# Transposes of h, of the memory and of most of x1 and x2 by whole VectorE instructions and a regrouping through DRAM; the first gate chunk's weights in pairs

## The chip, the cores and the metric

The kernel runs on one core of one Trainium2 chip. The metric is device microseconds (us) of one execution. TensorE does matrix products and transposes (PE in the profile, PEld for its weight loads); VectorE is DVE, ScalarE is ACT, GpSimd is POOL, and SyncE (SP) only issues transfers (SPq is its queue). SBUF is the memory on the chip, PSUM the accumulators of PE, DRAM the memory beside the chip.

## What is computed

One decoder layer on x (256 tokens, width 2048) with a memory of 256 tokens:

```python
x = x + 0.5 * swiglu(rms_norm(x, ffn1_norm), ffn1_gate, ffn1_up, ffn1_down)     # d_ff = 5632
proj = rms_norm(x, mix_norm) @ w_in                  # q, k, v of three groups of heads
mn = rms_norm(mem, mem_norm); mk, mv = mn @ w_mem_k, mn @ w_mem_v
x = x + concat(forgetting_attention, sliding_window_attention, memory_attention) @ w_out
x = x + 0.5 * swiglu(rms_norm(x, ffn2_norm), ffn2_gate, ffn2_up, ffn2_down)
# swiglu(x, g, u, d) = (silu(x @ g) * (x @ u)) @ d
```

All is float32. A product of activations and weights is made of three faster matmuls (type fp32r): both operands are split into a high part and the rest, and hi·hi, hi·lo and lo·hi are summed.

## The kernel before, in words

**Weights.** `project` makes one output chunk of 512 columns: for each pair of K tiles (2 x 128 rows, `KB = 2`) `load_w` takes a tile `raw` (4 buffers) and issues its load on SP (L218, 512 KB), ACT casts it to `hi` (L220, 3 buffers), DVE subtracts to get `lo` (L221, 3 buffers), and `mm_rows` issues 12 matmuls of 128x512 (L283 to L285). So a raw buffer comes free when DVE has made `lo`, and a hi buffer when PE has done with the pair three before. A load is issued four pairs ahead, a cast three.

**Activations.** A product needs its left side with the width on the partitions: x0T, memT, x1T, x2T (16 K tiles each, hi and lo) and hT (44 K tiles). For x0T, memT, x1T and x2T `transpose_chunk` makes a chunk of 4 K tiles: 8 PE transposes of 128x128 into PSUM (L240, tiles tp_...), then ACT and DVE scale by the norm's gain and split into hi and lo (L249, L250). For hT `quad_transposes` makes 16 DVE transposes of 32 partitions each (L263), then hi and lo follow (L225, L226).

**Order.** The program is written in the order of the products: first FFN (gate and up alternating over 11 chunks, names ga, ua; then down over 4 column chunks, da), the memory's projections mk and mv, the chunks of w_in (mq to fvb), w_out (wo, 4 column chunks), second FFN (gb, ub, db). Work beside the products is written as generators in `Lanes`; after every pair `lanes.tick()` lets each go on to its next `yield`, and the number yielded is how many ticks it waits. The compiler's scheduler then places instructions on each engine by its own estimates, so the order on an engine is not quite that of the code. The memory's transposes run in the down product, those of x1 in mk, those of x2 in w_out and the first gate chunk of the second FFN.

**Opening.** The first gate chunk (`project_first`) starts before x has arrived: K tiles 0 to 3 have one raw buffer each, the others go in pairs, and PE transposes of x0T stand between the products. Its order is written by hand.

Of the kernel before, what the change touches and what calls it, by code (L numbers as in the profile page):

```python
# [16 lines left out]
P = 128  # L17
# [63 lines left out]
def hybrid_layer(ctx, tc, x, mem, ffn1_norm, ffn1_gate, ffn1_up, ffn1_down, mix_norm, mem_norm,  # L81
# [23 lines left out]
    lanes = Lanes()  # L105

# [103 lines left out]
    def load_w(w, k0, nk, c0, width, name, raw=None):  # L210
        there = raw is not None
        if not there:
            raw = wpool.tile([P, KB, 512], F32, tag="raw", bufs=4, name=f"raw_{name}")
# [106 lines left out]
    def project_first(acc, aT, w, before, ready, name):  # L320


        batches = [(k, 1) for k in range(4)] + [(k, KB) for k in range(4, NK, KB)]

        def load(i):
            k, b = batches[i]
            before(k)
            return load_w(w, k, b, 0, 512, f"{name}_{k}", None if k else first_w)

        nxt = load(0)  # L330
        for i, (k, b) in enumerate(batches):
            (wh, wl), nxt = nxt, load(i + 1) if i + 1 < len(batches) else None
            ready(k)
            if k == 0:
                for a, v in ((0, wh), (1, wh), (0, wl)):
                    for t in range(NT):
                        nc.tensor.matmul(acc[:, t, :], aT[:, 0, a, t * P:(t + 1) * P], v[:, 0, :],
                                         start=a == 0 and v is wh, stop=False)
            else:
                for j in range(b):  # L340
                    mm_rows(acc, aT, k + j, wh[:, j, :], wl[:, j, :], False, k + j == NK - 1)
            lanes.tick()


    def ffn(xT, before, ready, stats, wg, wu, wd, after, last, name):


        with tc.tile_pool(name=f"h_{name}", bufs=1, reuse_waits="tile") as hpool, \
                tc.tile_pool(name=f"ht_{name}", bufs=2, reuse_waits="tile") as htmp:
            hT = hpool.tile([P, NF, 2, SEQ], F32R, name=f"hT_{name}")  # L350

            def transpose_h(j, h):
# [3 lines left out]
                for b in range(2):  # L356
                    f = slice(4 * j + 2 * b, 4 * j + 2 * b + 2)
                    split(hT[:, f, 0, :], hT[:, f, 1, :], raw[:, 2 * b:2 * b + 2, :])
                    yield 1

            rstd = None
            for j in range(DFF // 512):
                acc = psum("acc", f"g{name}{j}")
                if j == 0 and ready:
                    project_first(acc, xT, wg, before, ready, f"{name}g{j}")
# [14 lines left out]
                lanes.run(f"hT{name}{j}", transpose_h(j, g))  # L380
# [4 lines left out]

            for c in range(4):
# [65 lines left out]
    def mem_raw(c):  # L452
        raw = wpool.tile([P, NT, 512], F32, tag="raw", bufs=4, name=f"mraw{c}")
        nc.sync.dma_start(raw, memv[:, :, c * 512:(c + 1) * 512])
        return raw

    def mem_stages_T(c):
        def stages(tag):
            raw = mem_raw(c)
            yield 3  # L460
            yield from transpose_chunk(lambda: memTs[0], lambda: raw, 4 * c, 4, G_MEM, f"mem{c}")(tag)
            square_sums(ssm, raw, c)
        return stages

    def after1(c, t, c0, width):
        if t == 0:
            return
        if c == 0:
            memTs.append(r1.tile([P, NK, 2, SEQ], F32R, tag="r1", name="memT"))
        if c < 2:  # L470
            for i in (2 * c, 2 * c + 1):
                lanes.put(f"memT{i}", mem_stages_T(i), ("consts",))
        square_sums(ss1, xchunk(c), c)
# [5 lines left out]
    ffn(x0T, before0, ready0, stats0, gate1, up1, down1, after1, False, "a")  # L479
    memT = memTs[0]  # L480
    lanes.finish("memT3")


    with tc.tile_pool(name="mix", bufs=1, reuse_waits="tile") as mx, \
# [44 lines left out]
        lanes.finish("x1T3", "mk")  # L529
# [70 lines left out]
        def logits(tag, h0, qT, kT, fox, name):  # L600
# [89 lines left out]
        def mem_stages(tag, h0):  # L690
# [10 lines left out]
            s = mt.tile([P, 2, 512], F32, tag="s", name=f"ss_{name}")  # L701
# [78 lines left out]
        for c in range(4):  # L780
# [3 lines left out]
            else:  # L784
# [7 lines left out]
        lanes.finish("bT2")  # L792
# [12 lines left out]
    ffn(x2T, lambda k: lanes.finish("bT3") if k == 12 else None, None, stats2, gate2, up2, down2, store, True, "b")  # L805
# [31 lines left out]
```

## Time and profile before

| | us |
|---|---|
| median of 3 runs (1813.83 to 1814.91) | 1814.04 |
| the profiled execution | 1814.06 |
| its span in the trace | 1812.3 |
| PE busy | 1802.0 (99%) |
| DVE busy | 1091.0 (60%) |
| ACT busy | 845.0 (47%) |
| main DMA queue, share of 16 engines | 62.7% |

The span is from the first to the last instruction of the trace; the profiled execution's own time is 1.8 us longer. Busy times count an engine as busy from the start of an instruction to its end; matmuls overlap, so a PE that is busy all the time may still be slower or faster than another.

### The profile page before, as it was taken

The numbers are of one execution on the slowest core, as the hardware profiler recorded it, in microseconds if no ns is written. First come the engines' busy times: TensorE is split into PE (matmuls) and PEld (weight loads), VectorE is DVE, ScalarE is ACT, GpSimd is POOL, SyncE is SP. The second block draws the span as 40 slices with busy tenths as digits, with TensorE's granted clock in tenths as the row PEclk, the third lists the DMA queues.
The fourth block names the chain that finished last, engine by engine and source line by source line (L and its number), as shares of the span: only waits on it lengthen the run. The fifth ranks groups of instructions, "written<-read, shape, count | busy, mean of one in ns | idle before, by whom it ended". The sixth has DMA issues, their size and how long they took to land.

```text
span 1812.3 us, 21918 instructions
## 1 busy us (share of the span) xinstructions
PE 1802.0 (99%) x8258; PEld 1517.1 (84%) x8258; DVE 1091.0 (60%) x1483; ACT 845.0 (47%) x1149; POOL 10.8 (1%) x31
## 2 busy tenths in 40 slices
PE   8999999999999999999999999999999999999998
PEld 7888888888888888888999888888888888888887
DVE  5666666666655454645665455666666666654443
ACT  6444444444445443557666454444444444433332
POOL 2000000000000000000000000000000000000000
PEclk9999999999999999999999999999999999999999
DMA  7666666666666666465656556666666666656664
GB/s 233 194 191 195 196 190 195 195 191 194 193 194 208 191 213 197 164 174 158 181 153 186 175 179 193 190 194 194 189 193 194 196 196 195 191 195 205 204 205 128
DMA packets 183145, 344.54 MB, mean 190 GB/s; under 512 B 11194, under 2 KB 28928, under 8 KB 182912
## 3 DMA queue, kind: packets, MB, share of 16 engines
q1 hardware_dynamic: 181488, 340.49, 62.7%
q0 software_dynamic: 528, 1.22, 0.3%
q10 hardware_dynamic: 1024, 1.45, 0.3%
q8 instruction: 64, 1.05, 0.2%
q14 instruction: 41, 0.34, 0.1%
HBM read 341.01 MB, written 2.11 MB: 189 GB/s over the span
## 4 chain that ended last, share of the span: by engine, by line
PE 98%; DMA 1%; ACT 1%; DVE 1%; issue 0%; ACTq 0%; DVEq 0%
PE ua L284 4%; PE da L284 4%; PE da L283 4%; PE gb L284 4%; PE ub L283 4%; PE ub L284 4%; PE gb L283 4%; PE da L285 4%; PE ua L285 4%; PE gb L285 4%; PE ub L285 4%; PE ua L283 4%; PE db L285 4%; PE db L284 4%; PE db L283 4%; PE ga L283 4%
## 5 line engine op out<-in xcount | busy, mean ns | idle before, releaser
L221 DVE TENSOR_TENSOR lo_bd<-raw_bd,hi_bd 128x1024 fp32r<-128x1024 f32 x88 | 107.8, 1225 | 116.6 <-ACT hi_bd L220 116.5
L221 DVE TENSOR_TENSOR lo_ad<-raw_ad,hi_ad 128x1024 fp32r<-128x1024 f32 x88 | 107.8, 1225 | 111.2 <-ACT hi_ad L220 111.0
L221 DVE TENSOR_TENSOR lo_bu<-raw_bu,hi_bu 128x1024 fp32r<-128x1024 f32 x88 | 107.8, 1225 | 110.2 <-ACT hi_bu L220 110.2
L221 DVE TENSOR_TENSOR lo_au<-raw_au,hi_au 128x1024 fp32r<-128x1024 f32 x88 | 107.8, 1225 | 104.9 <-ACT hi_au L220 104.9
L220 ACT CAST hi_bd<-raw_bd 128x1024 fp32r<-128x1024 f32 x88 | 92.8, 1055 | 145.5 <-PE db L285 139.8
L220 ACT CAST hi_bg<-raw_bg 128x1024 fp32r<-128x1024 f32 x88 | 92.9, 1055 | 144.5 <-PE gb L285 87.0
L220 ACT CAST hi_ag<-raw_ag 128x1024 fp32r<-128x1024 f32 (+1 forms) x89 | 92.6, 1040 | 139.0 <-PE ga L285 83.2
L220 ACT CAST hi_ad<-raw_ad 128x1024 fp32r<-128x1024 f32 x88 | 92.7, 1053 | 131.9 <-PE da L285 108.0
L220 ACT CAST hi_bu<-raw_bu 128x1024 fp32r<-128x1024 f32 x88 | 92.7, 1054 | 105.6 <-PE ub L285 78.9
L220 ACT CAST hi_au<-raw_au 128x1024 fp32r<-128x1024 f32 x88 | 92.5, 1053 | 103.0 <-PE ua L285 79.1
L283 PE MATMUL da<-hi_ad,hT_a 128*128 128x512 f32 x352 | 137.5, 391 | 0.0
L284 PE MATMUL ua<-lo_au,x0T 128*128 128x512 f32 x352 | 137.2, 390 | 0.3 <-DVE lo_au L221 0.3
L284 PE MATMUL da<-lo_ad,hT_a 128*128 128x512 f32 x352 | 137.2, 390 | 0.0
L283 PE MATMUL gb<-hi_bg,x2T 128*128 128x512 f32 x352 | 137.2, 390 | 0.0
L285 PE MATMUL da<-hi_ad,hT_a 128*128 128x512 f32 x352 | 137.2, 390 | 0.0
L284 PE MATMUL gb<-lo_bg,x2T 128*128 128x512 f32 x352 | 137.1, 390 | 0.0
L285 PE MATMUL ua<-hi_au,x0T 128*128 128x512 f32 x352 | 137.1, 390 | 0.0
L285 PE MATMUL gb<-hi_bg,x2T 128*128 128x512 f32 x352 | 137.1, 390 | 0.0
L284 PE MATMUL ub<-lo_bu,x2T 128*128 128x512 f32 x352 | 137.1, 390 | 0.0
L285 PE MATMUL ub<-hi_bu,x2T 128*128 128x512 f32 x352 | 137.1, 390 | 0.0
L283 PE MATMUL ua<-hi_au,x0T 128*128 128x512 f32 x352 | 137.1, 390 | 0.0
L283 PE MATMUL ub<-hi_bu,x2T 128*128 128x512 f32 x352 | 137.1, 390 | 0.0
(476 smaller groups left out, 4008.7 us busy)
## 6 DMA issues: line engine op xcount, KB each, us to landing
raw_au<-in_ffn_up_dram SPq DMA_DIRECT2D x88, 512.0 KB, 4.5
raw_ad<-in_ffn_down_dram SPq DMA_DIRECT2D x88, 512.0 KB, 4.6
raw_bg<-in_ffn_gate_dram SPq DMA_DIRECT2D x88, 512.0 KB, 4.4
raw_bu<-in_ffn_up_dram SPq DMA_DIRECT2D x88, 512.0 KB, 4.4
raw_bd<-in_ffn_down_dram SPq DMA_DIRECT2D x88, 512.0 KB, 4.7
raw_ag<-in_ffn_gate_dram SPq DMA_DIRECT2D x86, 512.0 KB, 4.4
raw_wo<-in_w_out_dram SPq DMA_DIRECT2D x16, 512.0 KB, 3.8
raw_mk<-in_w_mem_k_dram SPq DMA_DIRECT2D x8, 512.0 KB, 3.4
```

The source lines that it names most:

```text
L220: nc.scalar.copy(h, r)
L221: nc.vector.tensor_tensor(out=l, in0=r, in1=h.bitcast(F32), op=ALU.subtract)
L283: nc.tensor.matmul(acc[:, t, :w], hi, wh, start=first, stop=False)
L284: nc.tensor.matmul(acc[:, t, :w], hi, wl, start=False, stop=False)
L285: nc.tensor.matmul(acc[:, t, :w], lo, wh, start=False, stop=last)
```

## The change

For hT (22 chunks), memT (4), x1T (4) and chunks 0 to 2 of x2T, a chunk of 256 tokens x 512 columns is turned in four steps. `turn_out`: two DVE transposes of 128x512, one for each 128 tokens, turn every 32x32 block in place and write the blocks side by side to `turn_out_...`; then four DMAs on SP (32 partitions, pieces of 512 bytes) write them to a DRAM tile `far_...`. `turn_in`: one DMA on SP reads them back to `turn_in_...` with rows of 2 KB, the width on the partitions. Then ACT and DVE scale and split from SBUF (`scaled`, or `split` for hT). Chunk 3 of x2T and all of x0T stay with PE. The memory's raw chunks move from the raw buffers of the weights to buffers of the FFN's own, and the memory's and three of x1's turns run beside the down product (`turns_a`).

In the opening, K tiles 0 to 3 now share two pair buffers (`first_w`, four loads on SP), are split one at a time, and the norm's gain goes first on ACT's queue; x's loads and transposes stand in another order (`XLOAD`, `XTRANS`).

```diff
-    first_w = wpool.tile([P, KB, 512], F32, tag="raw", bufs=4, name="first_w")
-    nc.scalar.dma_start(first_w[:, 0, :], gate1[0:P, 0:512])
     nc.scalar.dma_start(graw1, ffn1_norm[0].rearrange("(k p) -> k p", p=P))
     load_x(nc.scalar, 2, 2)
+    first_w = [wpool.tile([P, KB, 512], F32, tag="raw", bufs=4, name=f"first_w{i}") for i in range(2)]
+    for k in range(2 * KB):
+        nc.sync.dma_start(first_w[k // KB][:, k % KB, :], gate1[k * P:(k + 1) * P, 0:512])
+    load_x(nc.sync, 4, 2)
...
-    def quad_transposes(dst, src):
-
-        sv = src.rearrange("p t (k b s) -> p b t k s", b=4, s=32)
-        dv = dst.rearrange("p k (t a s) -> p a t k s", t=NT, s=32)
+    def turn_out(tmp, src, name):
+        for t in range(NT):
+            tc.keep_in_program_order(
+                nc.vector.transpose(
+                    out=tmp.rearrange("p (t b k s) -> p t k b s", b=4, t=NT, s=32)[:, t],
+                    in_=src[:, t, :].rearrange("p (k b f) -> p k b f", b=4, f=32)))
+        yield 2
+        far = dpool.tile([NT, 4, 32, 4, P], F32, name=f"far_{name}")
         for a in range(4):
-            for b in range(4):
-                tc.keep_in_program_order(
-                    nc.vector.transpose(out=dv[32 * b:32 * b + 32, a], in_=sv[32 * a:32 * a + 32, b]))
-                if b % 2:
-                    yield 1
+            nc.sync.dma_start(far[:, :, :, a, :].rearrange("t b f n -> f (t b) n"),
+                              tmp[32 * a:32 * a + 32, :].rearrange("f (c n) -> f c n", n=P))
+        yield 2
+        return far
+
+    def turn_in(dst, far):
+        return dst.rearrange("p (t n) -> p t n", t=NT), far.rearrange("t b f a n -> (b f) t (a n)")
...
+    def turn_chunk(xT, src, tile, k0, g0, name):
+        far = yield from turn_out(tile(f"out_{name}"), src, name)
+        raw = tile(f"in_{name}")
+        nc.sync.dma_start(*turn_in(raw, far))
+        yield 3
+        yield from scaled(xT, raw, k0, g0)
...
             def transpose_h(j, h):
 
-                raw = htmp.tile([P, 4, SEQ], F32, tag="raw", bufs=1, name=f"hr_{name}{j}")
-                yield from quad_transposes(raw, h)
+                far = yield from turn_out(turn_tile(f"out_{name}{j}"), h, f"{name}{j}")
+                raw = turn_tile(f"in_{name}{j}")
+                nc.sync.dma_start(*turn_in(raw, far))
+                yield 3
...
-            lanes.put(f"bT{c}", transpose_chunk(lambda: x2T, lambda c=c: xchunk(c), 4 * c, 4, G_FFN2,
-                                                f"x2_{c}"))
+            if c < 3:
+                lanes.run(f"bT{c}", turn_chunk(x2T, xchunk(c), turn_tile, 4 * c, G_FFN2, f"x2{c}"))
+            else:
+                lanes.put(f"bT{c}", transpose_chunk(lambda: x2T, lambda: xchunk(3), 12, 4, G_FFN2, "x2_3"))
```

The built order shows the change at three places. The first is SP's queue in a gate chunk of the first FFN (raw_ag_10 is the load of K tiles 10 and 11 of the gate's weights); before, the loads follow one another:

```order
L218 DMA raw_ag_10_689<-in_ffn_gate_dram 128x2x512
L218 DMA raw_ag_12_709<-in_ffn_gate_dram 128x2x512
L218 DMA raw_ag_14_729<-in_ffn_gate_dram 128x2x512
L218 DMA raw_au_0_753<-in_ffn_up_dram 128x2x512
L218 DMA raw_au_2_773<-in_ffn_up_dram 128x2x512
```

Now the four stores of the turned h and the load that reads them back stand between them:

```order
L218 DMA raw_ag_10_682<-in_ffn_gate_dram 128x2x512
L268 DMA far_a_639<-turn_out_a_600 32x8x128 x4
L218 DMA raw_ag_12_700<-in_ffn_gate_dram 128x2x512
L218 DMA raw_ag_14_718<-in_ffn_gate_dram 128x2x512
L410 DMA turn_in_a_680<-far_a_639 128x2x512
L218 DMA raw_au_0_742<-in_ffn_up_dram 128x2x512
L218 DMA raw_au_2_762<-in_ffn_up_dram 128x2x512
```

The loads of the pairs from raw_ag_12 on have come behind the stores, and those from raw_au_0 on behind the load that waits for the stores to land.

The second place is DVE at the end of the third column chunk of the first down product (da is that chunk's accumulator, lo_ad_2 the second weight pair of the next chunk). Before:

```order
L221 TENSOR_TENSOR lo_ad_0_5073<-raw_ad_0_5071,hi_ad_0_5072 128x1024
L221 TENSOR_TENSOR lo_ad_2_5091<-raw_ad_2_5089,hi_ad_2_5090 128x1024
L391 SCALAR_TENSOR_TENSOR x_sb<-da_4621,x_sb 128x512 x2
L221 TENSOR_TENSOR lo_ad_4_5109<-raw_ad_4_5107,hi_ad_4_5108 128x1024
L221 TENSOR_TENSOR lo_ad_6_5127<-raw_ad_6_5125,hi_ad_6_5126 128x1024
```

Now:

```order
L221 TENSOR_TENSOR lo_ad_0_5010<-raw_ad_0_5008,hi_ad_0_5009 128x1024
L450 SCALAR_TENSOR_TENSOR x_sb<-da_4552,x_sb 128x512 x2
L262 STREAM_TRANSPOSE turn_out_x_5026<-x_sb 128x4x4x32 x2
L221 TENSOR_TENSOR lo_ad_2_5031<-raw_ad_2_5029,hi_ad_2_5030 128x1024
L221 TENSOR_TENSOR lo_ad_4_5049<-raw_ad_4_5047,hi_ad_4_5048 128x1024
```

The two transposes of x1's chunk 2 have come in, and lo_ad_2, which stood ahead of the addition to x, has come behind both.

The third place is SP in the third column chunk of w_out (raw_wo_10 is the load of its sixth pair). Before:

```order
L218 DMA raw_wo_6_8480<-in_w_out_dram 128x2x512
L218 DMA raw_wo_8_8502<-in_w_out_dram 128x2x512
L218 DMA raw_wo_10_8520<-in_w_out_dram 128x2x512
L218 DMA raw_wo_12_8538<-in_w_out_dram 128x2x512
L218 DMA raw_wo_14_8556<-in_w_out_dram 128x2x512
```

Now, with the turns of x2's chunks 0 (far_x_8314) and 1 (far_x_8384):

```order
L218 DMA raw_wo_6_8389<-in_w_out_dram 128x2x512
L268 DMA far_x_8314<-turn_out_x_8275 32x8x128 x4
L218 DMA raw_wo_8_8411<-in_w_out_dram 128x2x512
L268 DMA far_x_8384<-turn_out_x_8343 32x8x128
L295 DMA turn_in_x_8364<-far_x_8314 128x2x512
L268 DMA far_x_8384<-turn_out_x_8343 32x8x128 x3
L218 DMA raw_wo_10_8435<-in_w_out_dram 128x2x512
L218 DMA raw_wo_12_8457<-in_w_out_dram 128x2x512
L295 DMA turn_in_x_8433<-far_x_8384 128x2x512
L218 DMA raw_wo_14_8475<-in_w_out_dram 128x2x512
L218 DMA raw_wo_0_8499<-in_w_out_dram 128x2x512
```

The first store of chunk 1, the load that reads chunk 0 back and three more stores have come ahead of raw_wo_10, and the load that reads chunk 1 back ahead of raw_wo_14.

## Rows read from the trace of the kernel before

**Rows 1.** Windows: length; busy us of PE, PEld, DVE, ACT, POOL; clock; DMA share; GB/s.
```profile
40.00:560.00 520.00, 520.00 (x2296) 430.97 (x2295) 338.86 (x413) 225.78 (x239) 0.00 (x0) 1.00 0.65 194
560.00:740.00 180.00, 180.00 (x815) 149.31 (x814) 92.28 (x108) 83.72 (x110) 0.00 (x0) 1.00 0.63 202
...
1020.00:1100.00 80.00, 80.00 (x372) 66.58 (x371) 47.74 (x63) 40.30 (x61) 0.00 (x0) 1.00 0.59 182
1100.00:1780.00 680.00, 680.00 (x3002) 563.66 (x3001) 413.60 (x477) 289.03 (x295) 0.00 (x0) 1.00 0.65 196
```

**Rows 2.** Timeline, ACT, in a gate chunk (start us, us, what [idle before]): weight casts.
```profile
60.78 1.05 ACT L220 CAST hi_ag<-raw_ag 128x1024 fp32r<-128x1024 f32 x1 [1.66 <-PE ga L285]
63.50 1.06 ACT L220 CAST hi_ag<-raw_ag 128x1024 fp32r<-128x1024 f32 x1 [1.67 <-PE ga L285]
```

**Rows 3.** The chain of waits (start us, us, what): blocks of PE transposes.
```profile
563.95 0.87 PE tp_mem L240 x8
...
739.21 0.87 PE tp_x L240 x8
...
1068.36 0.87 PE tp_x L240 x8
```

**Rows 4.** Groups by line, PE (busy us, mean ns | idle before): the memory's transposes.
```profile
L240 PE MATMUL tp_mem<-ident,mraw 128*128 128x128 f32 x32 | 4.1, 272 | 0.0
```

**Rows 5.** Groups by line and shape, DVE.
```profile
L221 DVE TENSOR_TENSOR lo_ag<-raw_ag,hi_ag 128x1024 fp32r<-128x1024 f32 x86 | 105.3, 1225 | 45.9 <-ACT hi_ag L220 44.9
L263 DVE STREAM_TRANSPOSE hr_a<-gsa 32x256 f32<-32x256 f32 x176 | 76.7, 436 | 3.2
...
L377 DVE SCALAR_TENSOR_TENSOR gsa<-ua,y_x,gsa 128x512 f32<-128x512 f32 x22 | 15.5, 747 | 4.5 <-PE ua L285 4.5
```

**Rows 6.** Groups by line and shape, ACT.
```profile
L225 ACT CAST hT_a<-hr_a 128x512 fp32r<-128x512 f32 x22 | 12.5, 618 | 0.0
...
L249 ACT ACTIVATE x2T<-tp_x,gT 128x256 fp32r<-128x256 f32 x16 | 7.4, 464 | 0.4
```

**Rows 7.** DMA issues (KB each, median us from issue to landing).
```profile
raw_ag<-in_ffn_gate_dram SPq DMA_DIRECT2D x86, 512.0 KB, 4.4
...
raw_mk<-in_w_mem_k_dram SPq DMA_DIRECT2D x8, 512.0 KB, 3.4
```

**Rows 8.** The tile out_dram: issues on SP (min/median/max ns); landing of the stores.
```profile
L799 SPq DMA_DIRECT2D out_dram<-x_sb x5: 356/357/361, 1628.5 to 1809.2; - x5
...
DMA to landing us min/median/max: 2.0/5.1/5.7
```

**Rows 9.** DMA queues: packets, MB, share of 16 engines.
```profile
q1 hardware_dynamic: 181488, 340.49, 62.7%
```

**Rows 10.** Timeline, DVE, at the end of the first down projection's third chunk.
```profile
676.69 1.29 DVE L391 SCALAR_TENSOR_TENSOR x_sb<-da,x_sb 128x512 f32<-128x512 f32 x2 [0.41 <-PE da L285]
677.89 1.22 DVE L221 TENSOR_TENSOR lo_ad<-raw_ad,hi_ad 128x1024 fp32r<-128x1024 f32 x1
```

**Rows 11.** Timeline, DVE, at the end of the first column chunk of w_out.
```profile
1033.94 1.23 DVE L788 TENSOR_TENSOR x_sb<-wo,x_sb 128x1024 f32<-128x1024 f32 x1 [0.41 <-PE wo L285]
```

**Rows 12.** The chain of waits in the first gate chunk.
```profile
1.29 4.40 DMA graw<-in_ffn_norm_dram
...
9.35 7.49 DMA raw_ag<-in_ffn_gate_dram
...
18.00 1.23 DVE lo_ag L221
```

**Rows 13.** Timeline, PE, in the first gate chunk and at its end.
```profile
7.36 2.04 PE L337 MATMUL ga<-hi_ag,x0T 128*128 128x512 f32 x4 [0.24 <-DVE x0T L246]
...
15.24 0.44 PE L240 MATMUL tp_x<-ident,x_sb 128*128 128x128 f32 x2 [0.32 <-DVE x0T L250]
...
19.68 0.44 PE L240 MATMUL tp_x<-ident,x_sb 128*128 128x128 f32 x2 [0.85 <-DVE x0T L250]
...
36.20 0.50 PE L284 MATMUL ua<-lo_au,x0T 128*128 128x512 f32 x1 [0.26 <-DVE lo_au L221]
```

More of the change, by code (lines that the diff above doesn't have):

```diff
@@ L208, in rsqrt, with load_w @@
         return yf
[L210 to L213, printed above, removed]
+    def load_w(w, k0, nk, c0, width, name):
+        raw = wpool.tile([P, KB, 512], F32, tag="raw", bufs=4, name=f"raw_{name}")
         hi = wpool.tile([P, KB, 512], F32R, tag="hi", bufs=3, name=f"hi_{name}")
@@ L318, in project_end, with project_first, split_one, batch @@
         lanes.tick()
[L320 to L341, printed above, removed]
+    def project_first(acc, aT, w, x_tiles, ordered, name):
+        pairs = [[wpool.tile([P, KB, 512], F32R, tag=tag, bufs=3, name=f"{tag}_{name}_{2 * i}")
+                  for tag in ("hi", "lo")] for i in range(2)]
+        def split_one(k):
+            h, l = (t[:, k % KB, :] for t in pairs[k // KB])
+            split(h, l, first_w[k // KB][:, k % KB, :])
+            return h, l
+        def batch(k):
+            if k in XLOAD:
+                load_x(nc.sync, *XLOAD[k])
+            return load_w(w, k, KB, 0, 512, f"{name}_{k}")
+        x_tiles(0)
+        wh, wl = split_one(0)
+        x_tiles(1)
+        for a, v in ((0, wh), (1, wh), (0, wl)):
+            for t in range(NT):
+                nc.tensor.matmul(acc[:, t, :], aT[:, 0, a, t * P:(t + 1) * P], v, start=a == 0 and v is wh,
+                                 stop=False)
+        one = split_one(1)
+        x_tiles(2)
+        mm_rows(acc, aT, 1, *one, False, False)
+        lanes.tick()
+        two, three = split_one(2), split_one(3)
+        mm_rows(acc, aT, 2, *two, False, False)
+        nxt = batch(4)
+        x_tiles(4)
+        mm_rows(acc, aT, 3, *three, False, False)
+        lanes.tick()
+        for k in range(4, NK, KB):
+            (wh, wl), nxt = nxt, batch(k + KB) if k + KB < NK else None
+            if k == 6:
+                ordered()
+            x_tiles(k + KB)
+            for j in range(KB):
+                mm_rows(acc, aT, k + j, wh[:, j, :], wl[:, j, :], False, k + j == NK - 1)
@@ L342, in project_first, with ffn @@
             lanes.tick()
-    def ffn(xT, before, ready, stats, wg, wu, wd, after, last, name):
+    def ffn(xT, before, first, stats, wg, wu, wd, after, beside, last, name):
         with tc.tile_pool(name=f"h_{name}", bufs=1, reuse_waits="tile") as hpool, \
@@ L363, in ffn @@
                 acc = psum("acc", f"g{name}{j}")
-                if j == 0 and ready:
-                    project_first(acc, xT, wg, before, ready, f"{name}g{j}")
+                if j == 0 and first:
+                    project_first(acc, xT, wg, *first, f"{name}g{j}")
                 else:
@@ L450, in hybrid_layer, with turns_a, beside_a @@
     memTs = []
[L452 to L459, printed above, removed]
+    def turns_a(htmp, turn_tile):
+        yield 10
+        lanes.finish("consts")
+        memTs.append(r1.tile([P, NK, 2, SEQ], F32R, tag="r1", name="memT"))
+        for c in range(4):
+            raw = htmp.tile([P, NT, 512], F32, tag="g", bufs=2, name=f"mraw{c}")
+            nc.sync.dma_start(raw, memv[:, :, c * 512:(c + 1) * 512])
             yield 3
-            yield from transpose_chunk(lambda: memTs[0], lambda: raw, 4 * c, 4, G_MEM, f"mem{c}")(tag)
+            yield from turn_chunk(memTs[0], raw, turn_tile, 4 * c, G_MEM, f"m{c}")
             square_sums(ssm, raw, c)
-        return stages
-    def after1(c, t, c0, width):
[L466 to L473, printed above, removed]
+        for c in range(3):
+            while c not in x1_there:
+                yield 1
+            fars.append((yield from turn_out(turn_tile(f"out_x1{c}"), xchunk(c), f"x1{c}")))
+    fars, x1_there = [], set()
+    def beside_a(htmp, turn_tile):
+        lanes.run("turns_a", turns_a(htmp, turn_tile))
+    def after1(c, t, c0, width):
+        if t == NT - 1:
+            x1_there.add(c)
+            square_sums(ss1, xchunk(c), c)
     def stats0():
@@ L519, in hybrid_layer, with turn_tile, turns_x1 @@
         x1T = mx.tile([P, NK, 2, SEQ], F32R, name="x1T")
-        for c in range(4):
-            lanes.put(f"x1T{c}", transpose_chunk(lambda: x1T, lambda c=c: xchunk(c), 4 * c, 4, G_MIX,
-                                                 f"x1_{c}"))
+        def turn_tile(n):
+            return mt.tile([P, 4 * SEQ], F32, tag="q" if n.startswith("out") else "s", name=f"turn_{n}")
+        def turns_x1():
+            raws = [turn_tile(f"in_x1{c}") for c in range(2)]
+            for c in range(2):
+                nc.sync.dma_start(*turn_in(raws[c], fars[c]))
+            far3 = yield from turn_out(turn_tile("out_x13"), xchunk(3), "x13")
+            for c in range(2):
+                yield from scaled(x1T, raws[c], 4 * c, G_MIX)
+                raws.append(turn_tile(f"in_x1{c + 2}"))
+                nc.sync.dma_start(*turn_in(raws[c + 2], (fars + [far3])[c + 2]))
+            for c in (2, 3):
+                yield from scaled(x1T, raws[c], 4 * c, G_MIX)
+        lanes.run("x1T", turns_x1())
         r1s = row_rstd(ss1, "x1")
```

77 lines of the change are left out of this document (44 added, 33 removed).

## The prediction

> **What bounds the kernel now.** I read the windows by stage first. In the gate and up chunks, the down product, w_out and the second FFN PE is busy in every microsecond, at a granted clock of 1.00 [rows 1]; DVE and ACT are busy half to two thirds of the time. A busy PE need not be at its pace, so I looked at a rhythm: in a gate chunk ACT casts a pair of weight tiles every 2.72 us and each time has waited 1.66 us for PE [rows 2]. One pair is 12 matmuls, so PE gives one per 0.227 us and everybody else waits for PE. The chain of waits agrees: it runs on PE, and the blocks of 8 PE transposes stand on it with 0.87 us each [rows 3]. So only PE work that goes away, and PE stalls that come or go, change the time. Bytes moved and DVE time count only where they reach PE.
>
> How much lateness reaches PE? Call T the moment at which PE releases a buffer of the weights. The cast then takes 1.05 us, the rest (lo) 1.23 us [rows 2, 5], so lo is there at T+2.3, while PE needs it two pairs later, at T+5.4: 3.2 us of slack. The raw tile's load goes out when the lo of four pairs earlier is done, 6 to 7 us before a cast needs the tile, and lands after a median of 4.4 us [rows 7]; with what is left there the whole pipe takes some 7 us of lateness of one load. Every question below is whether something exceeds one of these slacks.
>
> **PE transposes removed.** Memory 4, x1 4 and x2 3 chunks leave PE: 11 blocks of 8 at 0.87 us = **-9.6 us**. They are on the chain, and nothing takes their place on PE. The group's mean duration is 272 ns [rows 4], 2.5 times the 0.109 us that one adds to the chain, because neighbours overlap; the chain's step is the price. The Trainium skill ("TensorE: Matmul & The Clock Gate", Part 4: PE-mode transpose) gives about 275 ns in a kernel's context. The trace has that duration too, but not as time that the next instruction waits; charged in full, the 88 would be worth 24.2 us by it.
>
> **h's turns (22, one beside each gate and up chunk of 8 + 8 pairs, 43.5 us).** On DVE 16 transposes at 0.436 us = 7.0 us [rows 5] become two of 128x512. No row has that shape. The 128x512 operation with two inputs takes 0.75 us, and the old transpose moves 256 columns in 0.44, so I take 0.7 each (bounds 0.44, the old one's cost, to 0.87, twice it): 1.4 us. They stand in one piece behind the product of ua and gsa (2 x 0.75): DVE is closed for 2.9 us and the lo behind it is ready at about T+4.0 to 4.3, under 5.4. Price nothing; at 0.87 each still nothing.
>
> On SP four stores are issued at 0.36 us each [rows 8], then the load of turn_in waits until they have landed, and the weight loads from raw_au_0 on queue behind it. The output's stores of 256 KB land in a median of 5.1 us, at most 5.7, the one of 128 KB alone in about 2 [rows 8]; the new ones have 128 KB each, but in pieces of 512 bytes, which no row shows. With T the end of ua, they are issued from about T+2.8 to T+4.3. raw_au_0 is for the ninth pair, at T+21.8; with cast and lo its data must be there by T+19.7, its issue by T+15.3 (4.4 for the load). Two issues (turn_in and its own) lie between: the stores may take 15.3 - 0.7 - 4.3, about 10.2 us. ACT's two casts of hT (0.62 us each [rows 6]) stand ahead of hi_au_0: store and load together may take 19.7 - 1.2 - 0.4 - 4.3 = 13.8 us, where the load of 512 KB takes 3.4 to 4.4 [rows 7]. Expected: 5.1 to 5.7 plus 4.4, at most 10.1. So hidden, price nothing, 3.7 us left. Bandwidth: a turn moves 1 MB. The main queue moves 340.49 MB in 62.7% of 1812.3 us [rows 9], 0.30 MB per us: 3.3 us of all engines. By packets it is dearer: 16 x 0.627 x 1812.3 us over 181488 packets is 0.100 us each, and 1280 packets of a turn over 16 engines are 8.0 us. Either fits into the 35% that a stage of 43.5 us leaves free (15 us) [rows 1].
>
> Against this change speaks a rule of the Trainium skill ("VectorE: DVE Perf Modes", The three transpose paths, and the rules for kernel authors): a 128x128 transpose is best on TensorE, and a plain DMA that transposes by strides is 19 times slower than the crossbar's. Here DVE turns inside 32x32 blocks and the DMA's innermost run stays 512 contiguous bytes, so it is no element-wise stride; no run shows yet how such stores land, and the rule is the slow rival below.
>
> **The memory's and x1's turns.** They lie beside the down product and mk, with two or three pairs between their steps; by the same slacks no wait reaches PE there. One place differs, the second in the order: at the end of da's third chunk DVE now does the addition to x (1.29 us [rows 10]), two transposes (1.4) and only then lo_ad_2 (1.22): ready at T+3.9 where PE needs it one pair and one matmul after T, at 2.95. **+1.0 us** (0.3 with transposes of 0.44, 1.3 with 0.87). Before, lo_ad_2 stood ahead of the addition and had no such delay.
>
> **x2's turns.** Third place in the order. T is here the end of wo's first chunk. The addition of chunk 1 (1.23 us [rows 11]) can begin at T+8.2 (three pairs), lo_wo_4 (1.23) and two transposes follow: the first store of chunk 1 leaves at T+12.2. raw_wo_10 is queued behind it, behind the load of chunk 0 and three stores (five issues, 1.8 us): T+14.2, against about T+7.7 before. It lands at T+19, lo at 21.3; needed at 8.2 + 5 x 2.72 + 0.2 = 22.0. raw_wo_14 waits behind the second turn_in, so for the landing of chunk 1's stores, and ACT's four scalings (0.46 us each [rows 6]) go ahead of its cast; lo comes at T+27.4 where 27.4 is needed. I take **+0.2 us** (0 to 1.5; each us by which stores land later than 5.1 adds one). Chunk 2 lies 16 pairs from its need: nothing.
>
> **The opening.** Now the first matmul starts at 7.36, behind the gain's load (4.40 us from 1.29) [rows 12, 13], which goes out 0.5 us earlier in the change. Its first four matmuls run at 0.43 to 0.51 us each, half pace at the granted clock 1.00 [rows 13]. Then PE waits at 15.24 and at 19.68, 0.32 and 0.85 us by those rows and with the slow ends of the matmuls ahead some 2.0 us; the second goes back to raw_ag, issued at 9.35 because its buffer came free late, landing 7.49 us later, with ACT and DVE behind it [rows 12]. With K tiles 0 to 3 in two buffers, the loads of K tiles 4 and 6 can go out at about 5.3 and 7.2. A new wait comes at K tile 2 (some 0.55 us), where scalings of x0T stand ahead of its cast on ACT. I carry each start through: K tile 4 at about 15.4, K tile 8's transposes at 18.2 instead of 19.68, ua's first lo matmul at 34.3 instead of 36.20 [rows 13]: **-1.9 us** (0, if the earlier loads share the queue with x's and land no earlier, to -3.3, all stalls and the 0.5 us gone).
>
> **Sum.** 1814.06 - 9.6 - 1.9 + 1.0 + 0.2 = **1803.8 us**; the profiled execution is 0.02 above the median, so that needs no correction. The bounds of the terms make 1801 to 1807.
>
> **Rivals.** (1) Small waits beyond those priced, where slack is thinnest: stores landing 2 to 4 us later than 5.1 cost that much at raw_wo_10 and raw_wo_14 and tenths at the other places of x1 and x2, with the opening giving nothing: 1807 to 1810.4. For it speaks a landing of 7.49 us [rows 12], beside heavy traffic. (2) Nothing gained: the load of turn_in holds SP a little too long in each of h's chunks; 0.3 to 0.6 us in each of 22 eats the 10 us: 1810.4 to 1817.7. Against it stand the 3.7 us left. (3) Slower: the same place, stores slow in 512-byte pieces. It begins above 10.2 us to land, or 13.8 with the load, has eaten all the gain 0.5 us beyond (22 x 0.5 = 11 us), and at a landing of 12 us costs (12 + 4.4 - 13.8) x 22 = 57 us: about 1861. For it: no row has such pieces; against it, the packet price above, taken as the dearest, makes 4 stores (1024 packets) 6.4 us of 16 engines, still under 10.2. (4) The transposes are worth their full duration: 88 x (0.272 - 0.109) = 14 us more [rows 3, 4], 1789. Against it the chain's step.
>
> **How the numbers follow.** The forecast's own case (1801 to 1807) 0.70, rival 1 0.13, rival 2 0.08, rival 3 0.07, rival 4 0.02. The time is that of the likeliest. About 0.2%, 3.6 us, is what a measurement of this kernel can tell from no change: faster (under 1810.4) 0.70 + 0.13 + 0.02 = 0.85, same 0.08, slower 0.07. The range takes the first two cases, 1801 to 1810.
>
> **What the profile of the changed kernel would show.** Right: no tp_mem and tp_x in the down product and mk; the windows from 40 us on still with PE at 100% except at da's fourth chunk, where PE waits about 1 us for lo_ad_2; STREAM_TRANSPOSE of 128x512 at about 0.7 us, DVE's busy time lower by 22 x 5.6 = 123 us; stores of far landing in at most 5.7 us, turn_in in 4.4; the DMA share above 62.7%; ua's first lo matmul at 34.3. Wrong: PE waiting in each up chunk for hi_au_0 with turn_in behind it; far landing above 10 us; transposes above 1.5 us each, which would stall PE behind ua's end and at each boundary of the down product; a pace of PE other than 2.72 us a pair.

## The result and the profile after

The changed kernel takes **1804.16 us** (median of 4, 1803.99 to 1805.28), the kernel before 1813.93 beside it: a ratio of 0.9946, 95% interval 0.9929 to 0.9964. The forecast was 1803.8. Its terms, read from the two traces:

| term | forecast, us | in the traces, us |
|---|---|---|
| 11 blocks of PE transposes gone | -9.6 | -9.7 (11 x 0.886) |
| opening (first up chunk's second matmul) | -1.9 | -1.6 (36.20 to 34.59; 33.50 to 35.33 in the other kernels with this opening and an early gain) |
| h's 22 turns | 0 | 0.0 (down product begins at 493.06, now 491.46: still 1.6 earlier) |
| da's fourth chunk waits for lo_ad_2 | +1.0 | +1.0 |
| w_out waits for lo_wo_10 | +0.2 | +0.9 |

They add up to -9.4; the profiled execution's span is 10.0 us shorter (1812.3 to 1802.3). Some 0.3 us of the rest is a short wait of PE in the first down product before (638 us) that is gone; 0.3 us is spread over stages without a place of its own. What a block is worth is read from the steps of PE around it: from the last matmul ahead to the third one behind there are 0.886 us more than three steps at the pace, 0.87 for the block and the rest for the matmul behind it, which starts late.

The windows of the changed kernel (as in [rows 1]):

```profile
40.00:560.00 520.00, 520.00 (x2296) 430.58 (x2295) 279.75 (x267) 228.71 (x246) 0.00 (x0) 1.00 0.73 221
560.00:740.00 180.00, 179.25 (x791) 148.11 (x790) 99.72 (x122) 84.36 (x110) 0.00 (x0) 1.00 0.74 230
1020.00:1100.00 80.00, 79.40 (x355) 65.48 (x354) 51.44 (x69) 42.85 (x62) 0.00 (x0) 1.00 0.75 228
```

In the gate and up chunks PE is as busy as before and DVE has 59 us less to do; in the other two windows PE lost 0.75 and 0.60 us. The shapes that no row of before had, first DVE's group for h in the first FFN:

```profile
L262 DVE STREAM_TRANSPOSE turn_out_a<-gsa 128x512 f32<-128x512 f32 x22 | 14.2, 687 | 0.0
```

0.69 us a transpose, where 0.7 was taken. Then the DMA queue and the issues (count, KB each, median us to landing):

```profile
q1 hardware_dynamic: 226512, 375.36, 68.8%
...
far_a<-turn_out_a SPq DMA_DIRECT2D x44, 128.0 KB, 2.6
turn_in_a<-far_a SPq DMA_DIRECT2D x11, 512.0 KB, 5.7
...
far_x<-turn_out_x SPq DMA_DIRECT2D x28, 128.0 KB, 3.1
turn_in_x<-far_x SPq DMA_DIRECT2D x7, 512.0 KB, 5.1
```

Stores in 512-byte pieces land in 2.6 us, half of what was reckoned with, the load in 5.7, 1.3 more than a weight tile in [rows 7]; together 8.3 where 13.8 were free. The main queue is busy for 68.8% of the span (62.7 in [rows 9]). ACT's timeline at the end of a gate chunk shows how little is seen of it:

```profile
113.58 1.05 ACT L220 CAST hi_ag<-raw_ag 128x1024 fp32r<-128x1024 f32 x1 [1.67 <-PE ga L317]
114.53 1.14 ACT L225 CAST hT_a<-turn_in_a 128x512 fp32r<-128x512 f32 x2
116.30 1.06 ACT L220 CAST hi_au<-raw_au 128x1024 fp32r<-128x1024 f32 x1 [0.63 <-PE ga L317]
```

The casts of hT follow the cast of a weight pair without a wait, and the cast after them (hi_au_0) still waits 0.63 us for PE.

### The profile page after: what moved, and what is told of

It is laid out like the page before. It is cut to its first block, busy times and chain, and to the rows that moved or that the text cites. A ratio compares the mean times of both kernels' runs of the same rounds, so it can differ in the third digit from the quotient of the medians.

```text
span 1802.3 us, 21677 instructions
## 1 busy us (share of the span) xinstructions
PE 1792.4 (99%) x8170; PEld 1507.2 (84%) x8170; DVE 976.4 (54%) x1197; ACT 845.7 (47%) x1149; POOL 12.1 (1%) x31
## 3 DMA queue, kind: packets, MB, share of 16 engines
q1 hardware_dynamic: 226512, 375.36, 68.8%
## 4 chain that ended last, share of the span: by engine, by line
PE 98%; DVE 1%; ACT 1%; DMA 0%; issue 0%; POOL 0%; DVEq 0%; POOLq 0%; ACTq 0%
PE ua L316 4%; PE ua L317 4%; PE gb L317 4%; PE ub L317 4%; PE gb L315 4%; PE ub L315 4%; PE gb L316 4%; PE ub L316 4%; PE ua L315 4%; PE da L316 4%; PE db L316 4%; PE db L315 4%; PE da L317 4%; PE db L317 4%; PE da L315 4%; PE ga L316 4%
## 5 line engine op out<-in xcount | busy, mean ns | idle before, releaser
L221 DVE TENSOR_TENSOR lo_bg<-raw_bg,hi_bg 128x1024 fp32r<-128x1024 f32 x88 | 107.4, 1220 | 96.4 <-ACT hi_bg L220 95.6
L221 DVE TENSOR_TENSOR lo_ag<-raw_ag,hi_ag 128x1024 fp32r<-128x1024 f32 x86 | 104.9, 1220 | 93.8 <-ACT hi_ag L220 92.9
L220 ACT CAST hi_ag<-raw_ag 128x1024 fp32r<-128x1024 f32 x86 | 90.7, 1055 | 135.9 <-PE ga L317 83.2
L317 PE MATMUL ua<-hi_au,x0T 128*128 128x512 f32 x352 | 136.9, 389 | 0.0
L315 PE MATMUL ub<-hi_bu,x2T 128*128 128x512 f32 x352 | 136.9, 389 | 0.0
```

Source lines behind the costliest of these rows:

```text
L315: nc.tensor.matmul(acc[:, t, :w], hi, wh, start=first, stop=False)
L317: nc.tensor.matmul(acc[:, t, :w], lo, wh, start=False, stop=last)
```

## The experiments

The times of the kernel before beside them were 1813.6 to 1813.7 us.

**The opening alone.** The kernel before with `first_w`, `project_first`, `XLOAD` and `XTRANS` of the changed one.

```diff
-    nc.scalar.dma_start(first_w[:, 0, :], gate1[0:P, 0:512])
     nc.scalar.dma_start(graw1, ffn1_norm[0].rearrange("(k p) -> k p", p=P))
+    first_w = [wpool.tile([P, KB, 512], F32, tag="raw", bufs=4, name=f"first_w{i}") for i in range(2)]
...
-    XLOAD = {3: (4, 2), 4: (6, 2), 6: (8, 4), 8: (12, 4)}
+    XLOAD.update({6: (6, 2), 8: (8, 4), 10: (12, 4)})
```

> The kernel before with the new opening alone (first gate chunk's K tiles in pairs, new order of x's loads); all transposes as before. Theory A, the terms of the sum are separate and each is a change on PE: in the trace of the changed kernel the first up chunk's second matmul starts at 34.59 us instead of 36.20, so 1.6 us less: 1812.3 us. Rival B, the opening's gain is only there because the later parts changed too, or is given back later: 1813.9 us.

Measured: **1811.93 us** (median of 10; ratio 0.9988, interval 0.9979 to 0.9998), 1.7 less, and the second matmul of ua at 34.58 us. The opening's term is separate and is not given back.

**h as before.**

```diff
-                far = yield from turn_out(turn_tile(f"out_{name}{j}"), h, f"{name}{j}")
-                raw = turn_tile(f"in_{name}{j}")
-                nc.sync.dma_start(*turn_in(raw, far))
-                yield 3
...
+                raw = turn_tile(f"hr_{name}{j}").rearrange("p (k s) -> p k s", k=4)
+                yield from quad_transposes(raw, h)
```

> The changed kernel with h alone turned as before, by 16 VectorE transposes of 32 partitions each and no way through DRAM. Theory A, h's turns are hidden both ways: 1804.2 us within 0.3, though VectorE is busy 22 x 5.6 = 123 us longer and the main queue moves 23 MB less. Rival B, the lighter VectorE brings part of the gain: above 1805.5 us. Rival C, the way through DRAM costs something that the other terms cover: below 1803.5 us.

Measured: **1803.82 us** (1802.66 to 1805.30), and its window of the gate and up chunks:

```profile
40.00:560.00 520.00, 520.00 (x2296) 430.59 (x2295) 342.59 (x421) 227.88 (x246) 0.00 (x0) 1.00 0.67 198
```

DVE is busy 62.8 us more than in the changed kernel there, the DMA share is 6 points lower, and PE is busy throughout with the same 2296 matmuls. A sharper measure than the median, whose runs spread over 2.6 us, is the time in the trace from ua's first lo matmul to the first matmul of the down product. The first line below is of the kernel before, the second of the changed kernel, the last two of this run:

```profile
493.06 0.39 PE L283 MATMUL da<-hi_ad,hT_a 128*128 128x512 f32 x1
...
491.46 0.39 PE L315 MATMUL da<-hi_ad,hT_a 128*128 128x512 f32 x1
...
34.86 0.50 PE L327 MATMUL ua<-lo_au,x0T 128*128 128x512 f32 x1 [0.28 <-DVE lo_au L221]
...
491.73 0.39 PE L326 MATMUL da<-hi_ad,hT_a 128*128 128x512 f32 x1
```

With ua at 36.20 before and 34.59 in the changed kernel it is 456.9 us in all three. h's turns, the most numerous part of the change, bring nothing and cost nothing.

**Three times the traffic for h.** These lines stand twice, for i = 0 and 1.

```diff
+                hop = dpool.tile([NT, 4, 32, 4, P], F32, name=f"hop{i}_{name}{j}")
+                nc.sync.dma_start(hop.rearrange("t b f a n -> (t b f) (a n)"),
+                                  far.rearrange("t b f a n -> (t b f) (a n)"))
+                far = hop
                 raw = turn_tile(f"in_{name}{j}")
                 nc.sync.dma_start(*turn_in(raw, far))
```

> The changed kernel with two more copies from DRAM to DRAM between h's stores and the load of turn_in, so the 22 turns move 3 MB each instead of 1 and arrive two landings later; the built order then puts the load and hT's casts some pairs further back. Theory A, traffic and landing beside the products are free as long as what waits for them stands behind enough casts: 1804.2 us within 0.5, with the main queue's share of time up from 68.8% by about 6. Rival B, the traffic is near its limit and slows the weight loads: 1 us or more in each of 22 turns, above 1826 us.

Measured: **1804.24 us** (1802.67 to 1804.94). Window and issues:

```profile
40.00:560.00 520.00, 520.00 (x2296) 430.58 (x2295) 278.78 (x267) 227.92 (x246) 0.00 (x0) 1.00 0.78 243
...
hop_a<-far_a SPq DMA_DIRECT2D x11, 512.0 KB, 5.6
...
turn_in_a<-hop_a SPq DMA_DIRECT2D x11, 512.0 KB, 4.7
```

Two landings of about 5 us more and a DMA share of 0.78 in place of 0.73 reach PE nowhere. (The main queue's share over the span rose by 2.7 points, not 6: a copy counts once there, so its bytes rose from 375.36 to 398.43 MB, while the memory's reads and its writes rose by 23.1 MB each.) It doesn't show where the limit lies: the built order put the casts of hT three pairs further back, so the wait for them grew along with the delay.

**x1 on PE again.** x1's four chunks through `transpose_chunk` in mk, and no turns of x1 beside the down product.

```diff
...
-        lanes.run("x1T", turns_x1())
+        for c in range(4):
+            lanes.put(f"x1T{c}", transpose_chunk(lambda: x1T, lambda c=c: xchunk(c), 4 * c, 4, G_MIX,
+                                                 f"x1_{c}"))
```

> The changed kernel with x1 alone transposed on TensorE as before, in the mk chunk. Theory A, a block of 8 costs its 0.87 us on the chain: 4 x 0.87 = 3.5 us more, and the wait of 1.0 us at the fourth column chunk of the first down product goes, while the wait of 0.3 us that the kernel before had in that product may come back: 1806.7 to 1807.0 us. Rival B, the block costs the transposes' own 272 ns each: 4 x 8 x 0.272 - 1.0 = 7.7 more, 1811.9 us.

Measured: **1807.07 us** (1806.45 to 1807.53), 2.9 more where 4 x 0.886 - 1.0 = 2.5; the wait at da's fourth chunk is gone. In its profiled execution w_out waited 2.2 us and the opening was 1.1 shorter, so agreement within a few tenths is partly luck; 7.7 it is not.

**h on PE.**

```diff
...
+                    for k in range(4):
+                        for t in range(NT):
+                            nc.tensor.transpose(tp[:, k, t * P:(t + 1) * P], h[:, t, k * P:(k + 1) * P], ident)
                     yield 1
+                    for b in (0, 2):
+                        f = slice(4 * j + b, 4 * j + b + 2)
+                        split(hT[:, f, 0, :], hT[:, f, 1, :], tp[:, b:b + 2, :])
```

> The changed kernel with h alone transposed on TensorE, 22 more blocks of 8, and split from PSUM. Theory A: 22 x 0.87 to 0.91 us (the matmul behind a block starts some 0.05 us late) = 19.1 to 20.0 more, 1823.3 to 1824.2 us. Rival B, 272 ns for each transpose: 22 x 2.18 = 47.9 more, 1852 us.

Measured: **1824.19 us** (1822.99 to 1825.03), 20.0 more; 22 x 0.886 is 19.5. Two of the 22 blocks on the chain of waits:

```profile
148.72 0.87 PE tp_ha L413 x8
...
193.14 0.87 PE tp_ha L413 x8
```

With 22 blocks added and 11 taken away, the price of a block on PE is settled: 0.87 on the chain, some 0.9 in all. The Trainium skill ("TensorE: Matmul & The Clock Gate", Part 4: PE-mode transpose) states about 275 ns for one 128x128 transpose of bf16 data in a kernel's context. The group of h_pe, in f32, has a mean of 272 ns too, but a step of 0.109 us from one to the next. Durations that overlap are no price.

**The two new waits taken away.** `wait`, between the transposes and the stores of turn_out, is 5 for x2's chunk 1 and 2 elsewhere.

```diff
+            yield 2
             fars.append((yield from turn_out(turn_tile(f"out_x1{c}"), xchunk(c), f"x1{c}")))
...
-        yield 2
+        yield wait
```

> The changed kernel with the turns of x1 begun two pairs later and the stores of x2's chunk 1 three pairs later, so that lo_ad_2 no longer stands behind the addition and two transposes, nor raw_wo_10 behind chunk 1's stores. Theory A, the two waits in the trace (1.0 us at the fourth chunk of the first down product, 0.9 to 2.3 us in w_out in the traces so far) come from these two orders and from nothing else: both are gone from the trace, 1801.5 to 1802.3 us. Rival B, lateness only moves to the next load or cast: 1803.5 us or more.

Measured: **1802.01 us** (1801.96 to 1802.27, ratio to before 0.9935, 0.9923 to 0.9948), 2.15 less than the changed kernel. The windows:

```profile
560.00:740.00 180.00, 180.00 (x796) 149.10 (x795) 100.84 (x126) 85.16 (x111) 0.00 (x0) 1.00 0.74 231
1020.00:1100.00 80.00, 80.00 (x358) 66.29 (x357) 51.63 (x69) 43.51 (x64) 0.00 (x0) 1.00 0.75 230
```

PE has its 180 and 80 us again. Both waits came from these orders and did not move on.

**x2's chunk 3 turned as well,** on top of the fix, where its use follows 6 pairs later; its two tiles are raw buffers of the weights.

```diff
+            if c == 3:
+                lanes.run("bT3", turn_chunk(x2T, xchunk(3), lambda n: wpool.tile(
+                    [P, KB, 512], F32, tag="raw", bufs=4, name=f"turn_{n}").rearrange("p a b -> p (a b)"),
+                    12, G_FFN2, "x23", 1))
...
```

> The kernel of the fix with x2's chunk 3 turned by VectorE and DRAM too, so that nothing is left of the block of PE transposes there; here no product covers the turn: on ACT three scalings that wait for the load of turn_in stand ahead of the cast of the third weight pair of the next chunk. With T the end of w_out: addition and transposes to T+2.7, stores issued to 4.6 and landed at 7.2 (2.6 as measured), load landed at 13.1 (5.5), cast and lo at 16.7, where PE needs it at 5.7. Theory A: one block less (0.9) and a wait of 11 us: about 1812 us. Rival B, the landings are shorter where the queue is empty (4 us for the load): 1809 us. Rival C, the pipe's slack hides it: 1801 us.

Measured: **1811.66 us** (median of 10), 9.65 more than the fix; the size was right, the place only in part. Windows, SP's queue and PE:

```profile
1076.00:1080.00 4.00, 0.46 (x3) 0.10 (x1) 3.63 (x4) 0.00 (x0) 0.00 (x0) 0.84 0.08 17
1080.00:1084.00 4.00, 4.00 (x10) 3.13 (x11) 0.00 (x0) 0.00 (x0) 0.00 (x0) 0.50 0.97 223
...
1078.77 1.85 SPq L268 DMA_DIRECT2D far_x<-turn_out_x  x4
1080.67 0.48 SPq L218 DMA_DIRECT2D raw_bg<-in_ffn_gate_dram  x1
1082.91 0.38 SPq L295 DMA_DIRECT2D turn_in_x<-far_x  x1
...
1079.91 0.80 PE L316 MATMUL gb<-lo_bg,x2T 128*128 128x512 f32 x1 [3.54 <-DVE lo_bg L221]
1080.50 0.63 PE L317 MATMUL gb<-hi_bg,x2T 128*128 128x512 f32 x1
```

SP, which issues nothing else, stood from 1065.3 to 1078.8 us before the stores, which wait for the transposes; raw_bg_2, the load of the second pair, is queued behind them and was issued at 1080.7. So the second pair's cast waited for its own late load, where the third pair's had been reckoned to wait for the load of turn_in. PE lost 3.7 us waiting for the lo that stands behind addition and transposes, then 1.8, 1.0 and 0.9 us in three more waits, and between them ten matmuls went at steps of 0.43 us, 2 us more.

**The gain late.** The changed kernel with two lines exchanged.

```diff
-    nc.scalar.dma_start(graw1, ffn1_norm[0].rearrange("(k p) -> k p", p=P))
     load_x(nc.scalar, 2, 2)
+    nc.scalar.dma_start(graw1, ffn1_norm[0].rearrange("(k p) -> k p", p=P))
```

> The changed kernel with the norm's gain behind x's second load on ACT's queue, as before. Theory A, the opening's gain is that of the earlier loads of K tiles 4 and 6; the earlier start itself (0.89 us) is mostly lost again in the wait at K tile 2, which ACT's and DVE's work ends: first matmul some 0.5 us later, time 1804.2 to 1804.5 us. Rival B, the opening's gain is that of the start: 1804.7 to 1805.1 us.

Measured: **1805.88 us** (1805.50 to 1806.28), 1.7 more than the changed kernel. Both theories had less than that. PE:

```profile
6.12 0.26 PE L142 MATMUL gps<-ident,graw 16*128 16x16 f32 x1 [1.26 <-DMA graw<-in_ffn_norm_dram]
...
7.66 2.04 PE L374 MATMUL ga<-hi_ag,x0T 128*128 128x512 f32 x4 [0.24 <-DVE x0T L246]
...
35.88 0.50 PE L316 MATMUL ua<-lo_au,x0T 128*128 128x512 f32 x1 [0.28 <-DVE lo_au L221]
```

The gain's load holds PE for 1.26 us; everything up to ua (35.88) is late by the same 1.3 us. The wait in w_out was 1.2 us in this execution, 0.3 more than in the changed kernel's, which makes up most of the rest.

**The gain first, alone.** The kernel before with two lines exchanged.

```diff
-    nc.scalar.dma_start(first_w[:, 0, :], gate1[0:P, 0:512])
     nc.scalar.dma_start(graw1, ffn1_norm[0].rearrange("(k p) -> k p", p=P))
+    nc.scalar.dma_start(first_w[:, 0, :], gate1[0:P, 0:512])
```

> The kernel before with two lines exchanged: the norm's gain goes first on ACT's queue, ahead of the first weight tile; all else as before. The changed kernel with the gain late took 1.7 us more, so the start counts when K tiles go in pairs; this run shows whether it counts alone. Theory A, the start is worth nothing while the later loads bind (PE's waits at 15.24 and 19.68 us in the trace of before stay where they are): 1813.3 to 1813.6 us. Theory B, the opening's gain is the start's alone: 0.9 to 1.2 us, 1812.4 to 1812.7 us, with the first up chunk's second matmul at 35.0 to 35.3 instead of 36.20.

Measured: **1813.10 us** (median of 10; ratio 0.9996, interval 0.9987 to 1.0006), 0.6 less, which the interval doesn't tell from nothing. PE:

```profile
6.91 1.20 PE L337 MATMUL ga<-hi_ag,x0T 128*128 128x512 f32 x4 [0.73 <-DVE x0T L250]
...
14.55 0.44 PE L240 MATMUL tp_x<-ident,x_sb 128*128 128x128 f32 x2 [0.90 <-DVE x0T L250]
...
19.10 0.44 PE L240 MATMUL tp_x<-ident,x_sb 128*128 128x128 f32 x2 [0.98 <-DVE x0T L250]
...
35.61 0.50 PE L284 MATMUL ua<-lo_au,x0T 128*128 128x512 f32 x1 [0.26 <-DVE lo_au L221]
```

The first product starts 0.45 us earlier than in [rows 13], where it now waits for the first weight tile, which landed at 6.21 us. In this execution its four matmuls also took 1.20 us instead of 2.04. The two later waits grew, from 0.32 and 0.85 to 0.90 and 0.98 us, and ua gained 0.6.

**K tiles 2 and 3 of x0T one at a time,** on top of the fix, and both kernels once more.

```diff
-    XTRANS = {0: (0, 1), 1: (1, 1), 2: (2, 2), 4: (4, 2), 6: (6, 2), 8: (8, 4), 12: (12, 4)}
+    XTRANS = {0: (0, 1), 1: (1, 1), 2: (2, 1), 3: (3, 1), 4: (4, 2), 6: (6, 2), 8: (8, 4), 12: (12, 4)}
...
-        two, three = split_one(2), split_one(3)
+        two = split_one(2)
+        x_tiles(3)
+        three = split_one(3)
```

> The kernel of the fix with x0T's K tiles 2 and 3 transposed and scaled one at a time, so that the cast of K tile 2's weights stands behind one scaling instead of two. Theory A, the wait at K tile 2 (0.34 us beyond the pace in the changed kernel's trace, at 11.46 us) comes from that order: 0.2 to 0.4 us less, 1801.6 to 1801.8 us. Rival B, the wait only moves to K tile 3: 1802.0 us.

> The kernel of the fix once more beside that of the new order of K tiles 2 and 3, on one chip. In the traces so far PE's first matmuls run at 0.43 us a step for a time that differs from execution to execution, and the five times of the other kernel fall into 1801.0 and 1802.5 to 1802.8. Theory A, that time at half pace sets the spread and not the order: this kernel too shows times near 1801 in some executions; if it is at full pace from the first weight matmuls on, its first up chunk's second matmul stands near 33.5 instead of 34.6 to 34.8. Rival B, the order of K tiles 2 and 3 brings the gain: all times stay at 1802.0 to 1802.3.

> The kernel with x0T's K tiles 2 and 3 one at a time, once more, beside the fix. Theory A, the half pace sets the time: 1801.0 in some executions and about 1802.5 in others, median within 0.5 us of the fix. Rival B, the order brings 0.3 to 1.0 us: median 1801.0 to 1801.7 with the fix at 1802.0.

Measured: the new order 1800.99 (1800.96 to 1802.82), then 1801.66 (1800.95 to 1803.00); the fix 1802.01, then 1802.03 (1801.26 to 1802.29). In the first profiled execution of the new order PE began so:

```profile
6.47 1.17 PE L374 MATMUL ga<-hi_ag,x0T 128*128 128x512 f32 x4 [0.29 <-DVE x0T L246]
```

Four matmuls in 1.17 us, where the changed kernel's took 2.04; its ua began at 33.50. In the second profiled execution the four took 2 us again, and ua began at 34.97. x1_pe has the old order, and in its profiled execution the four matmuls ran as fast:

```profile
6.48 1.17 PE L374 MATMUL ga<-hi_ag,x0T 128*128 128x512 f32 x4 [0.24 <-DVE x0T L246]
...
33.50 0.50 PE L316 MATMUL ua<-lo_au,x0T 128*128 128x512 f32 x1 [0.27 <-DVE lo_au L221]
```

Its ua began at 33.50 too. So the wait at K tile 2 doesn't set the difference, and these traces show no gain of the new order; the pace of the first matmuls goes with 1.1 us in the old order and 1.5 in the new. Over ten executions each, the new order's median is 0.65 us below that of the fix (1801.4 and 1802.0) in ranges that overlap, so a gain of some tenths isn't ruled out.

## Why the prediction was right, and where it was not

**What bounds the kernel.** Right: PE's pace of 2.72 us a pair sets nearly everything from 40 us on. Work given back to DVE and traffic removed (h as before) and traffic added (three times) change nothing; PE work added or removed changes the time by its step on the chain. (ACT is busy 42 to 50% of the windows of [rows 1], a little less than the half to two thirds read there.)

**The price of a block.** Right, at 0.87 against 0.886 measured; rival 4, the full duration, is refuted by h on PE (20 us, not 48).

**h's turns at nothing.** Right, with more room than forecast: the stores' landing was over-sized at 5.1 to 5.7 us (2.6 measured), the load's under-sized at 4.4 (5.7). Rivals 2 and 3 have nothing behind them. The Trainium skill ("VectorE: DVE Perf Modes", The three transpose paths) warns that a plain DMA which transposes by strides is 19 times slower than the crossbar's when the innermost stride of the destination is large. These stores, with 512 contiguous bytes innermost, don't test that; shorter pieces were not tried.

**The wait at da's fourth chunk.** Right, in place and size, and in cause, as the fix shows:

```profile
671.18 1.29 DVE L450 SCALAR_TENSOR_TENSOR x_sb<-da,x_sb 128x512 f32<-128x512 f32 x2 [3.01 <-PE da L317]
672.38 1.30 DVE L262 STREAM_TRANSPOSE turn_out_x<-x_sb 128x512 f32<-128x512 f32 x2
673.60 3.46 DVE L221 TENSOR_TENSOR lo_ad<-raw_ad,hi_ad 128x1024 fp32r<-128x1024 f32 x3
...
674.84 0.50 PE L316 MATMUL da<-lo_ad,hT_a 128*128 128x512 f32 x1 [0.76 <-DVE lo_ad L221]
```

The add, two transposes and the lo follow one another on DVE, and PE idles 0.76 us beyond the modelled end of its last matmul. By the steps this matmul is 0.9 us late and the one behind it another 0.1.

**The wait in w_out.** Right in place, mis-sized: 0.2 forecast with a bound of 1.5, 0.9 measured, and 1.2 to 2.2 in the traces of five other kernels with that order. SP, ACT and PE:

```profile
1031.21 0.86 SPq L218 DMA_DIRECT2D raw_wo<-in_w_out_dram  x1
1037.32 0.30 SPq L268 DMA_DIRECT2D far_x<-turn_out_x  x1
1037.84 0.38 SPq L295 DMA_DIRECT2D turn_in_x<-far_x  x1
1038.26 1.55 SPq L268 DMA_DIRECT2D far_x<-turn_out_x  x3
1039.86 1.35 SPq L218 DMA_DIRECT2D raw_wo<-in_w_out_dram  x2
1044.07 0.37 SPq L295 DMA_DIRECT2D turn_in_x<-far_x  x1
...
1042.03 1.71 ACT L286 ACTIVATE x2T<-turn_in_x,gT 128x256 fp32r<-128x256 f32 x4 [1.77 <-DMA turn_in_x<-far_x]
1045.74 1.05 ACT L220 CAST hi_wo<-raw_wo 128x1024 fp32r<-128x1024 f32 x1 [2.00 <-DMA raw_wo<-in_w_out_dram]
...
1048.10 0.50 PE L316 MATMUL wo<-lo_wo,mixT 128*128 128x512 f32 x1 [0.60 <-DVE lo_wo L221]
```

The add that starts at T+8.2 starts at 1033.72, so T is 1025.5. The first store of chunk 1 leaves at 1037.3 (T+11.8) and raw_wo_10 at about 1039.9 (T+14.4): both as reckoned. But its cast begins at 1045.74, 5.9 us after the issue, where 4.8 had been put in; a load and four stores go out in the 2.6 us ahead of it. What made it land late was not tried by itself.

**The opening.** The sum was right (-1.6 to -1.7 against -1.9), and so were the places carried through: K tile 4 at 15.49 us (15.4 forecast), K tile 8's transposes at 18.33 (18.2). The parts were not. The loads of K tiles 4 and 6 went out at 3.70 and 6.33 us, not 5.3 and 7.2, and the start, to which 0.5 us was given, came 0.89 earlier: the gain's load, issued at 0.81, no longer holds PE, which goes on from its idle matmuls straight to the transposes:

```profile
5.12 1.11 PE L240 MATMUL tp_x<-ident,x_sb 128*128 128x128 f32 x4
6.47 2.04 PE L374 MATMUL ga<-hi_ag,x0T 128*128 128x512 f32 x4 [0.24 <-DVE x0T L246]
...
12.02 0.50 PE L316 MATMUL ga<-lo_ag,x0T 128*128 128x512 f32 x1 [0.17 <-DVE lo_ag L226]
...
34.59 0.50 PE L316 MATMUL ua<-lo_au,x0T 128*128 128x512 f32 x1 [0.27 <-DVE lo_au L221]
...
7.00:9.00 2.00, 2.00 (x6) 1.54 (x5) 1.44 (x3) 0.62 (x1) 0.74 (x2) 1.00 1.09 392
```

Together the two parts are worth 1.7 us. The gain's place alone brought 0.6, within the noise. The pairs alone, with the gain late, were not run on the kernel before: 1.74 less the 1.72 measured on the changed kernel leaves nothing, and by ua in graw_late (35.88 against 36.20) they bring 0.3. The reading that fits: with single K tiles an earlier start mostly lengthens the later waits, and with pairs those waits are gone but the late gain sets the start, two limits in a row of which each part lifts one. It is argued from single traces, and ua differs by up to 1.8 us between the traces of kernels with the same opening. The wait at K tile 2 came where forecast, at 0.34 us beyond the pace instead of 0.55; the traces of h_old and the fix show none there. The last row is the window from 7 to 9 us, with its six matmuls at steps of 0.43 us. The working called this half pace at a granted clock of 1.00, which was a misreading, as the last section shows.

**The chances.** The case forecast (1801 to 1807) came in, and rival 1's mechanism, a landing later than reckoned at raw_wo_10, came in at 0.7 us, too little to move the case.

## What to carry to other kernels

Where one engine sets the pace, price a removed operation by its step on the chain, and check all other parts only against the slack of the pipe that feeds that engine. A way through DRAM of some 11 us (transposes, stores, load) costs nothing where the order leaves it that long, and an order of two instructions costs a microsecond where it doesn't: look at what is queued behind a wait on the in-order queue, SP's first of all. If two parts each lift one of two limits in a row, each may show little alone; test both with and without the other.

## What was not expected of the hardware

In the opening PE's matmuls go at steps of 0.43 us instead of 0.23 until a moment that differs from execution to execution. In x1_pe the first product, at 6.5 us, already has the full pace; in the changed kernel the pace rises at about 10.1 us, in graw_late at 12.5. The windows there, the last row of the opening above for one, print a granted clock of 1.00, but that is no reading. The trace's records of the clock begin only at 6.32 us in x1_pe, 9.35 in the kernel before, 10.12 in the changed kernel and 12.51 in graw_late, each time about where the slow steps end, and a window without a record is printed as 1.00. In all_turned PE had stood still for 3.5 us, the steps behind that were 0.43 us as well, and there a record gives a granted clock of 0.50 (the lower level, 1.2 GHz). So the slow steps of the opening look like the lower level too, though no record covers them. One wait in the middle of the kernel cost 2 us on top of itself. A store of 128 KB from 32 partitions in pieces of 512 bytes landed in 2.6 us (median of 44), a copy of 512 KB from DRAM to DRAM in about 5.
